# Half-product units in a hybrid encoder step: weight sums on GpSimd alone, stored sums on the vector engine, one load queue, more buffers for the last merges

## The chip, the cores and the metric

One core of a Trainium2 chip runs the whole program. The metric is the device time of one execution in microseconds; the median of several executions is compared. In the text PE is the tensor engine, DVE the vector engine, ACT the scalar engine, POOL GpSimd, and SP the engine that only issues transfers; SPq and ACTq are the instruction streams of SP and ACT where they issue transfers.

## The reference

One layer of a streaming encoder for a prompt of 1024 rows and 8 streams of 16 rows (T = 1152 rows together, width 1024). An input projection feeds two branches, a state-space branch (width 2048) and an attention branch (width 1024). The part that the change touches comes after both:

```
u   = gate_m * (y_m @ w_br_m) + gate_a * (y_a @ w_br_a)      # y_m: T x 2048, y_a: T x 1024
out = u @ w_out                                              # T x 1024 @ 1024 x 1024
y   = layer_norm(alpha * x + out, ln_g, ln_b)
```

All of it is in float32 precision: each operand is split into a rounded high part and the remainder, and a product is three matmuls (high by high, high by low, low by high).

## The kernel before, in words

Everything is held transposed: channels on the 128 partitions, rows along the free axis, in three chunks of 384 rows (`ch(0)` to `ch(2)`). The last 415 us of the program, which the change touches, run in this order.

1. `quarter(A0, evac_0)`: the first half of the attention product, 24 outputs of 12 matmuls.
2. `unit(0, steps_0)`: the first half of the state-space product, by a scheme in the manner of Strassen. Its weights come in four pairs `p` (0 to 3; the second unit has 4 to 7). Each pair has four raw weight halves B11, B21, B12, B22 and four differences T1, T2, T4, T3 of them, so eight pieces; they are used in 11 products of 12 matmuls, into 9 PSUM banks, of which 8 can be open at a time.
3. `quarter(A1, evac_1)`: the second half of the attention product. Its results go to DRAM (`pa_d`). Beside it `load_sums(1)` scales the rows of the second unit and makes their sums.
4. `unit(1, steps_1)`: the second half of the state-space product. Its differences T are not made here: `sums_of_weights`, a generator that runs beside the first unit, made them, split them, and stored them in DRAM (`t_d`). Beside this unit, the generator `seconds` loads the two attention halves and their gate (`pa_d`, `gate_d`) for the chunks 0 and 1 and merges them; `final` loads the other gate (tile `gm`) and `finish` merges it into `acc`.
5. The output product with `w_out` and the normalisation: for chunk 0 the sum over `k` is outermost, and `late` merges chunk 2 of `acc` meanwhile, with loads by `load_late`; then chunks 1 and 2.

A piece is made ready by `prepare()`, one piece per step and three ahead of its use: for a raw half ACT casts the high part (L1484) and POOL subtracts for the low part (L1485); for a difference an engine subtracts first (`sum_of`, L1419); a stored difference is one DMA from `t_d` (L1481). The tiles `pc` rotate over four slots, so a piece can be cast only when PE is done with the piece four before. The raw halves sit in one tile `wu` (B11, B21) and two tiles `wv` (B12, B22), with no second buffer: the next pair is loaded (`load_pair`, L1407 and L1412) when the last reader of this pair is done. The list `coming` says at which piece a load is issued.

`sums_of_weights` does 16 steps. Each makes a difference on DVE (L1419), casts it on ACT (L1455), subtracts on DVE (L1442) and stores it from SP (L1439, `t_d<-te`). After them it loads the rows of the second attention half (`load_second`, L1467 and L1468), which `rows_c01` and `rows_c2` split (L1626, L1627).

What runs beside the products is paced by `Flow`: a generator yields a number of ticks, and PE's code calls `flow.tick()` twice per product, so a tick is six matmuls. Pacing decides only the order of instructions in each engine's stream; every engine then works through its stream in order, as its semaphores allow. Inside `with tc.manual_schedule():` each engine keeps the order in which the code issues; outside it a list scheduler orders the instructions by its own estimate of times. Before the change both units were inside such a block, `quarter(A1, ...)` and the statements between the second unit and the output product were not.

PSUM is read out by `to` and `put_on` (L1511 a copy by ACT for the first result of an `acc` block, L1513 and L1519 adds by DVE) and in the second unit by a copy into the tile `shared` (L1548).

Of the kernel before, what the change touches and what calls it, by code (L numbers as in the profile page):

```python
# [11 lines left out]
F32 = mybir.dt.float32  # L12
# [7 lines left out]
P = 128  # L20
# [129 lines left out]
def trunk_step(ctx: ExitStack, tc: tile.TileContext, I, O):  # L150
# [1250 lines left out]

    def load_pair(p, which):

        q = sy if p < 4 else ac
        if which == 0:
            t = wp.tile([P, 1024], F32, tag="wr", name=f"wu{p}", bufs=1)
            q.dma_start(t[:], weights_of(p, 0))  # L1407
            raw[p, "B11"], raw[p, "B21"] = t[:, 0:512], t[:, 512:1024]
        else:
            for i, n in enumerate(("B12", "B22")):  # L1410
                t = lazy["raw"].tile([P, 512], F32, tag=f"raw{i}", name=f"wv{p}_{i}", bufs=1)
                q.dma_start(t[:], weights_of(p, 1)[:, 512 * i:512 * i + 512])  # L1412
                raw[p, n] = t[:]
# [8 lines left out]
    def sums_of_weights():  # L1422

        early = {}

        def load(p):
            for j, names in enumerate((("B11", "B21"), ("B12", "B22"))):
                t = mp.tile([P, 1024], F32, tag="yr", name=f"we{p}_{j}", bufs=4)
                sy.dma_start(t[:], weights_of(p, j))
                early[p, names[0]], early[p, names[1]] = t[:, 0:512], t[:, 512:1024]  # L1430

        steps = [(p, i) for p in range(4, 8) for i in range(4)]
        made = {}
        load(4)
        yield 12
        for at in range(len(steps) + 2):
            if at >= 2:
                p, i = steps[at - 2]
                sy.dma_start(t_d[4 * (p - 4) + i], made[at - 2][1][:].bitcast(F32))  # L1439
            if 1 <= at <= len(steps):  # L1440
                x, o = made[at - 1]
                ve.tensor_tensor(o[:, 512:1024], x, o[:, 0:512].bitcast(F32), ALU.subtract)  # L1442
            if at < len(steps):
                p, i = steps[at]
                x = sum_of(early, p, SUMS[i], ve)
                o = ap.tile([P, 1024], F32R, tag=("ahi0", "alo0", "ahi1", "alo1")[i], name=f"te{p}_{i}")
                made[at] = (x, o)
                if i == 1:
                    if p < 7:
                        load(p + 1)  # L1450
                    else:
                        load_second(0)
                        load_second(1)
                yield 1.4
                ac.copy(o[:, 0:512], x)  # L1455
                yield 1.4
        load_second(2)
        load_second(3)
        yield 3

    rows2 = []

# [10 lines left out]
    def prepare():  # L1473

        n = len(pieces)
        if n >= lazy["limit"]:
            return
        p, name = n // 8, PIECES[n // 8][n % 8]
        t = wp.tile([P, 1024], F32R, tag=("wh", "wl")[n % 2], name=f"pc{n}")
        if p >= 4 and name in SUMS:  # L1480
            ac.dma_start(t[:].bitcast(F32), t_d[4 * (p - 4) + SUMS.index(name)])  # L1481
        else:
            out = sum_of(raw, p, name, ve if p else po) if name in SUMS else raw[p, name]
            ac.copy(t[:, 0:512], out)  # L1484
            po.tensor_tensor(t[:, 512:1024], out, t[:, 0:512].bitcast(F32), ALU.subtract)  # L1485
        pieces.append(t)
        if p % 4 < 3:
            for which, last, gap in ((0, "T4", 1), (1, "T3", 1)) if p < 4 else ((0, "B21", 2), (1, "B22", 3)):
                if name == last:
                    coming.append((n + gap, p + 1, which))  # L1490
        while coming and coming[0][0] <= n:
            load_pair(*coming.pop(0)[1:])
# [12 lines left out]
    def unit(v, steps):  # L1505
# [16 lines left out]
        for p in range(4):  # L1522
# [11 lines left out]
            for at, piece in enumerate(order):  # L1534
                prepare()
                if p == 3:
                    if at == 3:
                        fetch()
                    if at == 6:
                        split()  # L1540
# [93 lines left out]

    def steps_0(p, piece):

        if p == 3 and piece == "B12":
            flow.drain()
            lazy["rows"] = first_rows(1)
        if p == 3 and piece == "B22":  # L1640
            rows_c2()
# [14 lines left out]
        ac.copy(t, d)  # L1656
        ac.dma_start(pa_d[1, j][:, ch(c)], t)

    flow.start(load_sums(1, lazy["rows"]))
    quarter(A1, evac_1, lambda: unit_first(1))  # L1660
    flow.drain()

    G, U, wraw, pending, wo = {}, {}, {}, [], {}

    def seconds():

        xts = {}

        def load(j):
            G[j] = mp.tile([P, T], F32, tag="yr", name=f"pa{j}", bufs=4)  # L1670
            xt = xts[j] = ap.tile([P, 4 * CW], F32, tag=f"ahi{j % 2}", name=f"pb{j}")
            sy.dma_start(G[j][:, 0:2 * CW], pa_d[0, j][:, 0:2 * CW])
            sy.dma_start(xt[:, 0:2 * CW], pa_d[1, j][:, 0:2 * CW])
            sy.dma_start(xt[:, 2 * CW:], gate_d[8 + j][:, 0:2 * CW])

        load(0)
        load(1)
        yield 6
        for j in range(8):
            g, x, t = G[j][:, 0:2 * CW], xts[j][:, 0:2 * CW], xts[j][:, 2 * CW:]  # L1680
            yield 5
            ve.tensor_tensor(g, g, x, ALU.add)
            yield 1
            ve.scalar_tensor_tensor(g, t, 1.0, g, ALU.add, ALU.mult)
            if j < 6:
                load(j + 2)
            yield 5

    def final(*jcs):

# [13 lines left out]

    def load_late(j):

        for tag, src in (("gt", pa_d[0, j]), ("gt", pa_d[1, j]), ("s4", gate_d[8 + j]), ("s4", gate_d[j])):
            t = mp.tile([P, CW], F32, tag=tag, name=f"lt{j}", bufs=2)
            sy.dma_start(t[:], src[:, ch(2)])
            pending.append(t[:])  # L1710

    def late(j):

        x0, x1, ta, tm = (pending.pop(0) for _ in range(4))
        a = acc[:, j, ch(2)]
        po.tensor_tensor(x0, x0, x1, ALU.add)
        ve.scalar_tensor_tensor(x0, ta, 1.0, x0, ALU.add, ALU.mult)
        ve.scalar_tensor_tensor(a, tm, 1.0, a, ALU.add, ALU.mult)
        po.tensor_tensor(a, a, x0, ALU.add)
        if j < 7:  # L1720
            load_late(j + 1)

    def parts_of_u(c, ks):

# [58 lines left out]
    raw_stack.close()  # L1783
    op = ma_stack.enter_context(tc.tile_pool(name="op", bufs=1, reuse_waits="tile"))
    wo[0] = ready.pop(0)
    split_wo(2)
    lazy["seventh"]()
    split()
    wo[1] = ready.pop(0)
    load_wo(6)  # L1790
    parts_of_u(0, (3,))
    split_wo(3)
    parts_of_u(0, (4, 5))
    finish(2)
    load_late(0)
    rows_of_wo = (0, 2, 1, 3, 4, 5, 6, 7)
    gb = xp.tile([P, 2, D], F32, tag="xhi2", name="gb")
    sy.dma_start(gb[:, 0, :], I["ln_g"].to_broadcast([P, D]))
# [1 line left out]
    for c in range(NCH):  # L1800
# [20 lines left out]
        if c == 0:  # L1821
            for k in range(8):
                for j, n in blocks:
                    product(j, n, k)
                if k < 4:
                    split_wo(k + 4)
                if k == 0:
                    parts_of_u(0, (6, 7))
                if k == 2:
                    load_wo(7)  # L1830
                if k > 2:
                    late(k - 3)
            parts_of_u(1, range(8))
# [119 lines left out]
```

## Time and profile before

| | us |
|---|---|
| median of 3 executions | 2034.54 (2033.39 to 2042.21) |
| the profiled execution, its own time | 2032.59 |
| its span, first to last instruction | 2030.8 |
| PE busy | 2004.2 |
| DVE, ACT, POOL busy | 1358.9, 950.6, 545.5 |

Busy time of PE counts matmuls from a modelled start to a modelled end and says nothing on the rate inside; the number of matmuls in a stretch of time does. A row of the timeline gives the start in us, the duration in us, engine, line, operation, output and inputs, and in brackets how long the engine had been idle before it and what released it. SPq and ACTq rows are transfers being issued; their duration is the issue, not the transfer.

### The profile page before, as it was taken

What the parts mean: (1) busy time and instruction counts of PE and PEld (TensorE: products, weight loads), DVE (VectorE), ACT (ScalarE), POOL (GpSimd) and SP (SyncE); (2) the same over time, 40 slices, a digit from 0 to 9 for tenths busy, and PEclk for the clock granted to TensorE, in tenths of its full rate; (3) what the DMA queues carried; (4) which work ended last, traced back from release to release, by engine and by line L of the source; (5) the groups of instructions that cost most, each with busy time, mean ns of one, the idle gap of its engine ahead of it and who ended that gap; (6) DMA issues with size and microseconds to landing.
All of it is one profiled execution on the core that took longest, in us unless ns stands there. A gap on an engine that the chain in (4) does not pass through costs nothing. (4 is left out here: it accounts for less than half of the span.)

```text
span 2030.8 us, 36480 instructions
## 1 busy us (share of the span) xinstructions
PE 2004.2 (99%) x14199; PEld 1855.9 (91%) x14199; DVE 1358.9 (67%) x2229; ACT 950.6 (47%) x2059; POOL 545.5 (27%) x724
## 2 busy tenths in 40 slices
PE   9999999999999999999999999999999999899998
PEld 7899999999999999999898888988988999799977
DVE  4145666666767667643678777777786677765777
ACT  5125455564555655533555645545445463451310
POOL 0012535353535454423010010001001014413430
PEclk9999999999999999999999999999999999999999
DMA  7423242324332332334566656566566676677853
GB/s 222 166 66 94 69 136 79 131 77 124 95 126 83 127 99 99 124 123 145 167 191 197 201 206 201 186 220 199 174 214 209 216 255 227 206 241 274 286 165 125
DMA packets 139180, 332.37 MB, mean 164 GB/s; under 512 B 20360, under 2 KB 80256, under 8 KB 128768
## 3 DMA queue, kind: packets, MB, share of 16 engines
q1 hardware_dynamic: 117392, 226.17, 34.6%
q10 hardware_dynamic: 21616, 103.88, 14.8%
q8 instruction: 111, 1.82, 0.4%
q14 instruction: 61, 0.50, 0.1%
HBM read 255.66 MB, written 74.33 MB: 162 GB/s over the span
## 5 line engine op out<-in xcount | busy, mean ns | idle before, releaser
L247 PE MATMUL d<-xh,wh 128*128 128x384 f32 x2112 | 736.2, 349 | 0.0
L249 PE MATMUL d<-xh,wl 128*128 128x384 f32 x2112 | 708.3, 335 | 0.0
L248 PE MATMUL d<-xl,wh 128*128 128x384 f32 x2112 | 707.2, 335 | 0.0
L247 PEld LDWEIGHTS d<-xh,wh 128*128 128x128 f32 x2112 | 396.7, 188 | 19.0 <-issue 8.3
L248 PEld LDWEIGHTS d<-xl,wh 128*128 128x128 f32 x2112 | 397.2, 188 | 0.8
L249 PEld LDWEIGHTS d<-xh,wl 128*128 128x128 f32 x2112 | 396.5, 188 | 0.0
L227 POOL TENSOR_TENSOR wl<-wr,wh 128x1024 fp32r<-128x1024 f32 x37 | 90.6, 2447 | 182.9 <-ACT wh L226 182.9
L958 ACT ACTIVATE st<-s,ckt 128x256 f32<-128x256 f32 (+1 forms) x320 | 115.2, 467 | 18.7 <-PE s L953 16.4
L1018 ACT ACTIVATE st<-st 128x1024 f32<-128x1024 f32 x80 | 83.2, 1062 | 40.8 <-DVE st L1013 37.7
L962 POOL TENSOR_TENSOR st<-st,mask_bf 128x256 f32<-128x256 f32 x64 | 49.5, 794 | 194.5 <-ACT st L958 194.4
L707 ACT ACTIVATE m<-ce,nacum 128x128 f32<-128x128 f32 x288 | 96.9, 392 | 5.7 <-PE y L738 5.7
L230 DVE SCALAR_TENSOR_TENSOR wl<-wr,wh 128x1024 fp32r<-128x1024 f32 x50 | 63.7, 1274 | 32.5 <-ACT wh L229 32.4
L634 POOL TENSOR_TENSOR wx<-xdt,wdt 128x256 f32<-128x256 f32 x72 | 54.0, 751 | 84.8 <-DVE xdt L632 84.8
L226 ACT CAST wh<-wr 128x1024 fp32r<-128x1024 f32 x48 | 50.4, 1049 | 51.0 <-PE d L248 44.4
L1485 POOL TENSOR_TENSOR pc<-wu,pc 128x512 fp32r<-128x512 f32 x28 | 37.7, 1358 | 122.2 <-ACT pc L1484 122.2
L1028 PE MATMUL o<-st,vt 128*64 128x256 f32 (+1 forms) x640 | 68.4, 362 | 0.3
L1028 PEld LDWEIGHTS o<-st,vt 128*64 128x64 f32 x640 | 43.1, 137 | 25.8 <-issue 2.5
L853 ACT ACTIVATE gate<-d,bcol 128x384 f32<-128x384 f32 x48 | 27.7, 578 | 72.4 <-PE d L249 47.2
L687 POOL TENSOR_TENSOR S<-S,ea 128x256 f32<-128x256 f32 x56 | 37.8, 674 | 75.8 <-DVE S L688 64.6
L1039 DVE TENSOR_TENSOR st<-st 128x1024 f32<-128x1024 f32 (+1 forms) x40 | 57.4, 1435 | 0.8
L229 ACT ACTIVATE wh<-wr 128x1024 fp32r<-128x1024 f32 x50 | 52.7, 1054 | 10.8 <-PE d L248 10.8
L335 PE MATMUL v<-vh,xh 128*128 128x512 f32 x144 | 57.1, 397 | 0.0
(929 smaller groups left out, 4348.7 us busy)
## 6 DMA issues: line engine op xcount, KB each, us to landing
wr<-in_wt SPq DMA_DIRECT2D x88, 512.0 KB
kc<-in_cache_k ACTq DMA_DIRECT2D x32, 1024.0 KB
vc<-in_cache_v ACTq DMA_DIRECT2D x32, 1024.0 KB
ce<-ac_d SPq DMA_DIRECT2D x96, 192.0 KB
sb<-cs_d ACTq DMA_DIRECT2D x16, 576.0 KB
yr<-ym_d SPq DMA_DIRECT2D x16, 576.0 KB
gate_d<-gate SPq DMA_DIRECT2D x45, 192.0 KB
s<-in_state_ssm SPq DMA_DIRECT2D x8, 1024.0 KB
```

Source lines behind the costliest of these rows:

```text
L227: lazy.get("sub", po).tensor_tensor(lo[:, :cols], raw[:, :cols], hi[:, :cols].bitcast(F32), ALU.subtract)
L230: ve.scalar_tensor_tensor(lo[:, :cols], raw[:, :cols], scale, hi[:, :cols].bitcast(F32), ALU.mult, ALU.subtract)
L247: te.matmul(out, wh, xh, start=(k == 0), stop=False)
L248: te.matmul(out, wh, xl, start=False, stop=False)
L249: te.matmul(out, wl, xh, start=False, stop=(k == n - 1))
L335: te.matmul(d, xh, wh, start=(k == 0), stop=False)
L634: po.tensor_tensor(wx[b][:], xdt[b][:], wdt[:, b, hs][:, :, None].to_broadcast([P, 4, 64]), ALU.mult)
L707: ac.activation(m[:, j, :], ce[:, j * P:(j + 1) * P], AF.Abs, bias=nacum[:, b, h:h + 1])
L958: ac.activation(S[j][:, e, kb, q0:], ps2[:, e, 256 * x + q0:256 * x + 256], AF.Identity, bias=ckt[:, kb, 2 * hp + e:2 * hp + e + 1])
L1018: ac.activation(w, w, AF.Exp, scale=-1.0)
L1028: te.matmul(o[64 * e:64 * e + 64, 256 * at + q0:256 * at + 256], vt[:, kb, 64 * e:64 * e + 64], S[j][:, e, kb, q0:256], start=(kb == 0), s ...
L1039: ve.tensor_tensor(s[:, :, 0:h, :], s[:, :, 0:h, :], s[:, :, 2 * n - h:2 * n, :], ALU.add)
```

## The change

In the first unit: `sum_of` runs on POOL for every pair (before, for pairs 1 to 3 on DVE). In `sums_of_weights` the cast of the high part moves from ACT to DVE, directly behind the difference; the first wait falls from 12 to 8 ticks, a step from 2.8 to 2.6, and there are 5 ticks more after the last store. `flow.drain()` and `first_rows(1)` come after piece T2 of pair 3 instead of after B12, and the `fetch()` of the next weights one piece later.

In the second attention quarter: manual order.

In the second unit: the loads of raw halves and of the stored differences are issued by SP instead of ACT; the load of the next B11/B21 is issued two pieces later; `seconds` starts its loads 6 ticks later, then takes 9 ticks for a block instead of 11, and waits 2 ticks between the last read of a tile and the load that reuses it.

At the output: the statements between the unit and the product get manual order, and `load_late` has a second set of buffers, so that the loads of one merge are issued while the merge before it is at work.

```
     def load_pair(p, which):
-        q = sy if p < 4 else ac
+        q = sy
...
         load(4)
-        yield 12
+        yield 8
         for at in range(len(steps) + 2):
...
-                yield 1.4
-                ac.copy(o[:, 0:512], x)
-                yield 1.4
+                ve.tensor_copy(o[:, 0:512], x)
+                yield 2.6
+        yield 5
         load_second(2)
         load_second(3)
-        yield 3
+        yield 2
...
         if p >= 4 and name in SUMS:
-            ac.dma_start(t[:].bitcast(F32), t_d[4 * (p - 4) + SUMS.index(name)])
+            sy.dma_start(t[:].bitcast(F32), t_d[4 * (p - 4) + SUMS.index(name)])
         else:
-            out = sum_of(raw, p, name, ve if p else po) if name in SUMS else raw[p, name]
+            out = sum_of(raw, p, name, po) if name in SUMS else raw[p, name]
...
-            for which, last, gap in ((0, "T4", 1), (1, "T3", 1)) if p < 4 else ((0, "B21", 2), (1, "B22", 3)):
+            for which, last, gap in ((0, "T4", 1), (1, "T3", 1)) if p < 4 else ((0, "B21", 4), (1, "B22", 3)):
...
                 if p == 3:
-                    if at == 3:
+                    if at == 4 - v:
                         fetch()
...
     def steps_0(p, piece):
-        if p == 3 and piece == "B12":
+        if p == 3 and piece == "T2":
             flow.drain()
             lazy["rows"] = first_rows(1)
...
-    flow.start(load_sums(1, lazy["rows"]))
-    quarter(A1, evac_1, lambda: unit_first(1))
-    flow.drain()
+    with tc.manual_schedule():
+        flow.start(load_sums(1, lazy["rows"]))
+        quarter(A1, evac_1, lambda: unit_first(1))
+        flow.drain()
...
+        yield 6
         load(0)
         load(1)
-        yield 6
+        yield 4
         for j in range(8):
             g, x, t = G[j][:, 0:2 * CW], xts[j][:, 0:2 * CW], xts[j][:, 2 * CW:]
-            yield 5
+            yield 4
             ve.tensor_tensor(g, g, x, ALU.add)
             yield 1
             ve.scalar_tensor_tensor(g, t, 1.0, g, ALU.add, ALU.mult)
+            yield 2
             if j < 6:
                 load(j + 2)
-            yield 5
+            yield 2
...
     def load_late(j):
-        for tag, src in (("gt", pa_d[0, j]), ("gt", pa_d[1, j]), ("s4", gate_d[8 + j]), ("s4", gate_d[j])):
-            t = mp.tile([P, CW], F32, tag=tag, name=f"lt{j}", bufs=2)
-            sy.dma_start(t[:], src[:, ch(2)])
-            pending.append(t[:])
+        if j % 2:
+            x = wp.tile([P, 1024], F32, tag="wr", name=f"lx{j}", bufs=1)
+            at = [x[:, 0:CW], x[:, CW:2 * CW]] + [op.tile([P, CW], F32, tag=f"lt{i}", name=f"lt{j}_{i}")[:] for i in range(2)]
+        else:
+            at = [mp.tile([P, CW], F32, tag=("gt", "s4")[i // 2], name=f"lt{j}_{i}", bufs=2)[:] for i in range(4)]
+        for t, src in zip(at, (pa_d[0, j], pa_d[1, j], gate_d[8 + j], gate_d[j])):
+            sy.dma_start(t, src[:, ch(2)])
+            pending.append(t)
...                                      # late(j)
-        if j < 7:
-            load_late(j + 1)
+        if j < 6:
+            load_late(j + 2)
...
     wo[0] = ready.pop(0)
-    split_wo(2)
...
+    with tc.manual_schedule():
+        split_wo(2)
+        lazy["seventh"]()
+        split()
+        wo[1] = ready.pop(0)
+        load_wo(6)
+        parts_of_u(0, (3,))
+        split_wo(3)
+        parts_of_u(0, (4, 5))
+        finish(2)
+        load_late(0)
...
                 if k == 2:
                     load_wo(7)
+                if k == 1:
+                    load_late(1)
```

More of the change, by code (lines that the diff above doesn't have):

```diff
@@ L1785, in trunk_step @@
     wo[0] = ready.pop(0)
-    split_wo(2)
[L1787 to L1795, printed above, removed]
+    with tc.manual_schedule():
[9 more added lines that the diff above has]
+        load_late(0)
     rows_of_wo = (0, 2, 1, 3, 4, 5, 6, 7)
```

## Prediction

> **What bounds the kernel now.** First the page's head, then the windows by stage, then the list of waits of PE.
>
> ```profile
> span 2030.8 us, 36480 instructions
> ...
> PE 2004.2 (99%) x14199; PEld 1855.9 (91%) x14199; DVE 1358.9 (67%) x2229; ACT 950.6 (47%) x2059; POOL 545.5 (27%) x724
> ```
>
> PE is never free for long: 26.6 us of the span are without a matmul. So nothing can be won beside PE; only holes in PE's stream can close. The windows (columns: PE busy and matmul count, then PEld, DVE, ACT, POOL, granted clock, DMA share, GB/s) say where the holes are.
>
> ```profile
> 1615.40:1665.40 50.00, 50.00 (x291) 50.00 (x290) 41.16 (x64) 29.95 (x65) 2.54 (x2) 1.00 0.78 272
> 1665.40:1767.10 101.70, 94.86 (x529) 91.27 (x528) 70.01 (x95) 42.86 (x86) 49.84 (x35) 1.00 0.60 212
> 1767.10:1820.30 53.20, 50.61 (x290) 49.85 (x289) 43.33 (x62) 29.14 (x61) 11.60 (x6) 1.00 0.68 221
> 1820.30:1848.90 28.60, 24.85 (x134) 24.44 (x133) 9.62 (x16) 5.62 (x11) 5.14 (x4) 0.94 0.78 270
> 1848.90:1917.80 68.90, 68.90 (x398) 68.90 (x397) 46.19 (x70) 11.82 (x21) 28.70 (x22) 1.00 0.80 280
> ...
> 1665.40:1688.30 22.90, 22.90 (x133) 22.90 (x132) 9.92 (x15) 10.32 (x21) 15.66 (x12) 1.00 0.49 173
> ...
> 1917.80:1927.80 10.00, 7.30 (x26) 5.59 (x25) 8.54 (x12) 6.99 (x11) 3.42 (x3) 0.83 0.96 327
> 1927.80:1937.80 10.00, 8.28 (x35) 6.19 (x35) 10.00 (x11) 2.94 (x4) 5.53 (x4) 1.00 0.52 168
> 1937.80:1947.80 10.00, 10.00 (x46) 8.29 (x45) 6.89 (x11) 1.06 (x1) 2.50 (x3) 1.00 0.57 178
> ```
>
> Read as one stage a row: the first attention quarter (clean, 50.0 us), the first unit, the second quarter, the first pair of the second unit, its other three pairs (clean, 22.97 each); then pair 0 of the first unit (clean, 22.9), and three tens of the output product. Lost against the clean rate: the first unit 101.7 - 4 x 22.9 = 10.1; the second quarter 53.2 - 50.0 = 3.2; the second unit's first pair 28.6 - 22.97 = 5.6; the output 20 + 11 matmuls at 10/46 us = 6.7. Together 25.6 us. The whole prediction is how much of these four comes back.
>
> ```profile
> PE u10m L1499 <- ACT sh L1548: 3.8, 1, 3.8
> PE out L1818 <- DVE wl L230: 2.7, 1, 2.7
> PE dq L248 <- DVE ya1lo L1627: 2.2, 1, 2.2
> PE u02m L1499 <- ACT pc L1484: 1.8, 1, 1.8
> ...
> PE out L1817 <- ACT wh L229: 1.6, 1, 1.6
> ```
>
> Each loss has a name: pieces late in the first unit (`pc`), a late low part of the rows (`ya1lo`), one long wait at the start of the second unit, two late splits of `w_out`. The two longest cost more than the wait: after them the clock column falls (0.94, 0.83), and 5.6 us are lost for 3.8 waited.
>
> **First unit.** Four edits meet here: differences of pairs 1 to 3 on POOL (12 instructions move), 16 casts from ACT to DVE, the earlier start, the order of SP's loads.
>
> ```profile
> 1673.70 1.29 POOL L1419 TENSOR_TENSOR wu<-wv,wu 128x512 f32<-128x512 f32 x1
> 1675.73 1.29 POOL L1485 TENSOR_TENSOR pc<-wu,pc 128x512 fp32r<-128x512 f32 x1 [0.73 <-ACT pc L1484]
> 1676.98 1.29 POOL L1419 TENSOR_TENSOR wu<-wu 128x512 f32<-128x512 f32 x1
> ...
> 1755.59 1.27 POOL L1485 TENSOR_TENSOR pc<-wu,pc 128x512 fp32r<-128x512 f32 x1 [2.27 <-ACT pc L1484]
> ```
>
> Pair 0 already has its differences on POOL: one piece takes 1676.98 - 1673.70 = 3.28 us there (difference, cast by ACT, remainder). A pair then loads POOL with 15.7 of 22.9 us, and pair 0 lost nothing. So POOL itself fits. What made pairs 2 and 3 late shows on SP and DVE.
>
> ```profile
> 1729.25 9.98 SPq L1439 DMA_DIRECT2D t_d<-te  x4
> ...
> 1741.64 0.85 SPq L1412 DMA_DIRECT2D wv<-in_wbr  x2
> ...
> 1746.55 0.69 DVE L1419 TENSOR_TENSOR wu<-wv,wu 128x512 f32<-128x512 f32 x1 [3.55 <-DMA wv<-in_wbr]
> ```
>
> SP stands 10 us in the stores of the finished steps, because DVE is late with them, and the load of `wv` for pair 3 is queued behind the last store (1739.2) and the four row loads. It is issued at 1741.6 and in use at 1746.55; the third difference of that pair is ready at 1755.59 + 1.27 = 1756.9, and the unit ends 10.2 us later. So the unit ends 27.9 us after the last store, or after 91.6 us if that is later. The queue order is unchanged (row loads, then `wv`), and three pieces at 3.28 us on POOL take 9.8 us against 10.3 here, so the rule holds after: without loss the last store has to leave 63.7 us into the unit; before it was 73.8.
>
> When will it leave? Before, DVE's part:
>
> ```profile
> L1442 DVE TENSOR_TENSOR te<-we,te 128x512 fp32r<-128x512 f32 x16 | 17.4, 1090 | 10.8 <-ACT te L1455 10.5
> L1419 DVE TENSOR_TENSOR wu<-wv,wu 128x512 f32<-128x512 f32 x6 | 4.1, 682 | 3.8 <-DMA wv<-in_wbr 3.6 <-POOL pc L1485 0.3
> L1513 DVE TENSOR_TENSOR acc<-acc,u01m 128x384 f32<-128x384 f32 x10 | 5.0, 541 | 0.0
> L455 DVE TENSOR_SCALAR pl<-pl 128x432 f32<-128x432 f32 x7 | 2.7, 385 | 0.2
> ...
> 1704.33 1.29 POOL L1485 TENSOR_TENSOR pc<-wv,pc 128x512 fp32r<-128x512 f32 x1 [1.84 <-ACT pc L1484]
> ...
> 1704.35 1.81 DVE L1442 TENSOR_TENSOR te<-we,te 128x512 fp32r<-128x512 f32 x1
> ```
>
> Taken away: 10.5 us in which DVE stood waiting for ACT's casts, 12 differences of 0.68 us (8.2, of which about 9 fall before the last store: 6.1), and about 4 us by the start 4 ticks earlier (a tick is six matmuls, 1.04 us). Added: 16 copies. No row has a 128x512 copy on DVE; the nearest is one-input work on 128x432 at 0.385, which scales to 0.46, and two-input work of the same size is 0.68: 7.4 to 10.9 us; I take 0.46, since the copy has one input. Added too: waits for POOL. The last two rows show it: POOL starts at 1704.33, DVE's remainder 0.02 us later takes 1.81 instead of 0.68, that is, it ran when POOL was done. On average the remainders wait 1.09 - 0.68 = 0.41 us. POOL's share of the time rises from 49.84/101.7 to about 15.7/22.9, by 1.4, so 0.16 us more on each of 32 instructions (5 us), and 0.57 on each copy (9 us) if a copy waits as well, none if it doesn't. Sum: -10.5 - 6.1 - 4 + 7.4 + 5 + (0 to 9) = -8 to +1 us. I take the middle, -4. Ends for the range: -10 (all lost time), and +5, if POOL's waits double once more.
>
> The Trainium skill, "SBUF — State Buffer", section "Who interferes with whom", makes this a rule: a vector instruction with two SBUF inputs and a GpSimd instruction that reads SBUF hold a shared port pair in turn, each for its whole length, and a copy can enter the mode that needs the pair too. The trace agrees (1.81 against 0.68 us). By that rule the copies wait as well, and the sum here is the upper end, about +1 instead of -4.
>
> ACT loses 16 casts, and its in-order stream no longer ties the pieces to DVE; that is why I expect no new loss in pairs 1 and 2.
>
> **Second quarter.** Lost 3.2, of which 2.2 for `ya1lo`.
>
> ```profile
> 1756.88 0.33 SPq L214 DMA_DIRECT2D wr<-in_wbr  x1
> ...
> 1757.73 0.43 SPq L1341 DMA_DIRECT2D rsb<-rs_d  x1
> ...
> 1763.82 5.37 DVE L1345 SCALAR_TENSOR_TENSOR yr<-yr,mcol,rsb 128x1152 f32<-128x1152 f32 x2 [0.93 <-DMA rsb<-rs_d]
> ...
> 1773.00 3.07 DVE L1627 TENSOR_TENSOR ya1lo<-yc,ya1hi 128x384 fp32r<-128x384 f32 x2
> ...
> 1772.69 2.50 POOL L227 TENSOR_TENSOR wl<-wr,wh 128x1024 fp32r<-128x1024 f32 x1 [4.72 <-ACT wh L226]
> ```
>
> The rows' loads stood behind `fetch` (1756.88, held until the raw weights were free), so scaling began at 1763.82 and pushed `ya1lo` to 1773, where it also met POOL. After, the loads come two pieces earlier and ahead of `fetch`, and the casts of the last rows are issued ahead of the quarter's own. `fetch` moves behind two row loads and a broadcast, but it waits for the raw tile anyway. Forcing the order can also cost: ACT's read-outs stand in one line with the casts, but eight banks give 16 us. I take -2.5 (bounds -3.2 and +3, one wait of today's size doubled).
>
> **Second unit.**
>
> ```profile
> 1818.46 0.33 ACTq L1657 DMA_DIRECT2D pa_d<-pa  x1
> 1824.15 0.34 ACTq L1412 DMA_DIRECT2D wv<-in_wbr  x1
> ...
> 1828.60 0.44 ACTq L1481 DMA_DIRECT2D pc<-t_d  x1
> ```
>
> ACT stood 5.7 us at the issue of `wv`, whose tile was still being written to `pa_d`, and the first stored piece, the casts of the rows and the copy `sh` all came behind it: `pc<-t_d` left at 1828.60, PE needed it at 8.3 us into the unit (1828.6). After, SP issues these, ACT has its read-outs first, and `seconds` loads only 7 ticks later. The last store to `pa_d` can leave about 1 us after the quarter's end, so the piece leaves some 3 us into the unit and has 5 us to land, about what `wv` took above. I take -5.5 of 5.6. What is now queued on SP: every stored piece stands behind the merge loads and `gm` loads. A piece is issued three pieces, 8.3 us at least, ahead of use; a merge block is 1.2 MB, at 280 GB/s 4.2 us, and the piece itself 0.5 MB, 1.9 us. 6.1 of 8.3: the cover is 2.2 us, and if SP also waits for a free tile longer than that, PE waits. Blocks come every 9 ticks instead of 11, so DMA's 0.80 rises to about 0.85. Bounds: -5.6, and +6 (2 us at each of three pairs). The later load of B11/B21 has 6.3 us before its cast: nothing.
>
> **Output.**
>
> ```profile
> 1905.53 8.74 SPq L1737 DMA_DIRECT2D wor<-in_w_out  x2
> ...
> 1919.31 2.01 DVE L230 SCALAR_TENSOR_TENSOR wl<-wr,wh 128x1024 fp32r<-128x1024 f32 x1
> ...
> 1931.23 1.05 ACT L229 ACTIVATE wh<-wr 128x1024 fp32r<-128x1024 f32 x1
> ```
>
> The last merges of `seconds` (11 ticks a block) were drained in a lump, DVE was late, `wl` came at 1919.31 although PE was there at 1917.8; the next raw `w_out` could only be loaded after it, and its split at 1931.23 made the second hole. After, the last merge is issued at tick 79 instead of 84, 9 ticks a block; DVE has two instructions less in the last pair. Then `wl` is done before the unit ends and the load of the next raw tile has 8 us. I take -6 of 6.7, with -2 as the poor end. The second set of late buffers shortens merges that no hole in PE waits for: nothing, unless a bank is late; the last normalisation stays.
>
> **Sum.** -4 - 2.5 - 5.5 - 6 = -18. The profiled execution (2032.59; span 2030.8 and 1.8 around it) goes to 2014.6; its time lies 2.0 under the median, on which the forecast is made: 2034.5 - 18 = 2016.5.
>
> **Rivals.**
> 1. DVE and POOL take turns so often that the first unit gets nothing back or loses up to 5. For it: the 1.81 us row. Against: pair 0. Time 2034.5 - 14 + (0 to 5) = 2020.5 to 2025.5.
> 2. SP's single queue: stored pieces late in pairs 1 to 3. For: SP stood 8.74 and 9.98 us in single waits above; against: these pairs were clean with a DMA share of 0.80. +12 (4 us a pair): 2028.5, no measurable change. The same time comes if the forced order changes nothing because the waits move by a few us only.
> 3. Slower: DVE becomes the bound of the first unit by running out of banks. Its adds stand in line with the 48 instructions of the stored sums; nine banks are used in 22.9 us, so eight give it 20 us less the product's own 2, 18. If each of the 48 waits out a whole POOL instruction (1.29 + 0.6), a step takes 5.7 us and the adds of that time (10 of 0.54 us in 22.9) bring it to 7.4: 16 steps, 118 us, issued within 43; 118 - 43 - 18 = 57 us more than the clean 91.6, 47 more than before, and 2034.5 + 47 - 14 = 2067.5. It decides for slower by 10 us from 24 us net, a step of (24 + 10 + 43 + 18) / 16 = 5.9 us. Before, with the last store at 73.8 us, a step took at most 4.6.
>
> **How the numbers follow.** Half a per cent, 10 us, is about what a measurement of this kernel can tell from no change. The forecast's case (2007 to 2020): 0.57. Rival 1: 0.20, still faster. Rival 2 and no effect: 0.17, within. Rival 3: 0.06. So faster 0.77, same 0.17, slower 0.06. The lower end is all 25.6 us: 2009, less 2 for the spread of the median: 2007. The upper end takes rival 1 and part of rival 2: 2027.
>
> **What the profile after would show.** Right: no `pc` wait over 1 us in the first unit and the last `t_d<-te` leaving by 70 us into it; no wait of `u10m` and no clock under 1.00 in the second unit; `wl` done before the first `out`. Wrong: DVE remainders of 1.3 us and more throughout, adds 18 us behind their product; PE waiting for DMA `pc<-t_d` in pairs 5 to 7; a new wait of the quarter on ACT.

## The result, and the profile after

The changed kernel took 2026.99 us (median of 8 runs, 2024.26 to 2029.41) beside 2037.22 us for the kernel before on the same chip: ratio 0.9946, 95% interval 0.9931 to 0.9961. Measured once more (`e_after_again`) it took 2025.78 beside 2034.80: ratio 0.9959, 0.9946 to 0.9971. So 9 to 10 us were gained, where 18 were forecast. The median lies 0.01 us under the upper end of the forecast's range of 2007 to 2027. Head and busy time of the page after:

```profile
span 2025.7 us, 36480 instructions
...
PE 2004.6 (99%) x14199; PEld 1857.2 (92%) x14199; DVE 1371.2 (68%) x2233; ACT 944.6 (47%) x2043; POOL 566.0 (28%) x736
```

DVE has 12 us more work than before, POOL 20 more, ACT 6 less. The windows, one stage a row: first unit, second quarter, second unit, output (columns as before: PE, PEld, DVE, ACT, POOL, granted clock, DMA share, GB/s).

```profile
1667.70:1772.10 104.40, 96.89 (x530) 94.12 (x530) 87.75 (x103) 34.70 (x71) 71.08 (x47) 0.97 0.60 207
1772.10:1826.30 54.20, 51.74 (x290) 51.42 (x289) 40.67 (x59) 30.20 (x62) 10.90 (x5) 0.97 0.65 203
1826.30:1918.90 92.60, 92.07 (x529) 91.78 (x529) 59.27 (x88) 15.98 (x29) 35.88 (x28) 1.00 0.86 307
1918.90:2018.40 99.50, 99.03 (x482) 83.50 (x480) 75.51 (x135) 19.31 (x36) 23.67 (x19) 1.00 0.52 175
```

Against before: first unit 104.4 (101.7), quarter 54.2 (53.2), second unit 92.6 (97.5), output 99.5 (105.7). The two late stages gave what was forecast; the first unit and the quarter went the other way. What PE waits for:

```profile
PE u03d L1499 <- ACT pc L1484: 4.5, 1, 4.5
PE dq L249 <- POOL wl L227: 2.5, 1, 2.5
PE u02m L1501 <- POOL pc L1485: 2.1, 2, 1.1
...
PE u10m L1499 <- DMA pc<-t_d: 0.5, 1, 0.5
```

Of the long wait at `u10m` (3.8) 0.5 us are left; the waits at `ya1lo` (2.2) and `w_out` (2.7, 1.6) are gone. New are 4.5 us at `u03d`, the first piece of pair 3 of the first unit, and 2.5 us at the low part of the last weights of the quarter. The first one's cause stands in SP's stream and on ACT:

```profile
1728.68 10.91 SPq L1439 DMA_DIRECT2D t_d<-te  x4
1739.68 0.38 SPq L1407 DMA_DIRECT2D wu<-in_wbr  x1
...
1742.48 0.86 SPq L1412 DMA_DIRECT2D wv<-in_wbr  x2
...
1744.76 0.62 ACT L1484 CAST pc<-wu 128x512 fp32r<-128x512 f32 x1 [8.34 <-DMA wu<-in_wbr]
```

The load of pair 3's `wu` is queued behind the last four stores, and SP stands 10.9 us in these. Before, the same load was issued at 1728.81, ahead of them. The quicker pacing of `sums_of_weights` moved the stores forward in SP's stream, but DVE did not get quicker:

```profile
L1442 DVE TENSOR_TENSOR te<-we,te 128x512 fp32r<-128x512 f32 x16 | 18.0, 1122 | 0.2
L1454 DVE CAST te<-we 128x512 fp32r<-128x512 f32 x16 | 17.5, 1094 | 0.5
L1419 DVE TENSOR_TENSOR we<-we 128x512 f32<-128x512 f32 x8 | 9.8, 1230 | 0.0
L1419 DVE TENSOR_TENSOR we<-we,we 128x512 f32<-128x512 f32 x8 | 8.9, 1106 | 0.1
...
1711.84 1.39 DVE L1454 CAST te<-we 128x512 fp32r<-128x512 f32 x1
1715.98 0.43 DVE L1454 CAST te<-we 128x512 fp32r<-128x512 f32 x1
...
1711.51 2.87 POOL L1485 TENSOR_TENSOR pc<-wu,pc 128x512 fp32r<-128x512 f32 x2 [0.26 <-ACT pc L1484]
```

Of the two casts shown, the one beside an idle POOL took 0.43 us and the one beside a busy POOL 1.39; the mean of the 16 is 1.094. The stored sums cost DVE 54.2 us, and there is no idle time left among them.

### The profile page after: what moved, and what is told of

Its sections match the earlier page's. It is cut to its first block, busy times and chain, and to the rows that moved or that the text cites. A ratio compares the mean times of both kernels' runs of the same rounds, so it can differ in the third digit from the quotient of the medians.

```text
span 2025.7 us, 36480 instructions
## 1 busy us (share of the span) xinstructions
PE 2004.6 (99%) x14199; PEld 1857.2 (92%) x14199; DVE 1371.2 (68%) x2233; ACT 944.6 (47%) x2043; POOL 566.0 (28%) x736
## 4 chain that ended last, share of the span: by engine, by line
PE 83%; DVE 9%; DMA 2%; ACT 2%; issue 2%; POOL 1%; ACTq 0%; SPq 0%; DVEq 0%; POOLq 0%
PE d L247 17%; PE d L249 16%; PE d L248 16%; PE s L953 3%; PE o L1028 2%; PE y L738 2%; PE v L336 2%; PE v L337 2%; PE out L1826 2%; PE out L1827 2%; PE out L1825 2%; PE v L335 2%; PE so L1103 1%; PE dS L679 1%; PE y L742 1%
## 5 line engine op out<-in xcount | busy, mean ns | idle before, releaser
L958 ACT ACTIVATE st<-s,ckt 128x256 f32<-128x256 f32 (+1 forms) x320 | 115.5, 467 | 17.7 <-PE s L953 13.4
L226 ACT CAST wh<-wr 128x1024 fp32r<-128x1024 f32 x48 | 50.5, 1051 | 52.7 <-PE d L248 44.6
L944 POOL MEMSET st<- 128x256 f32 x32 | 9.9, 310 | 172.0 <-DVE fs L1042 172.0
```

The source lines that it names most:

```text
L958: ac.activation(S[j][:, e, kb, q0:], ps2[:, e, 256 * x + q0:256 * x + 256], AF.Identity, bias=ckt[:, kb, 2 * hp + e:2 * hp + e + 1])
```

## The experiments

Two theories went in. A: the first unit lost because the last stores, timed by a DVE that waits for POOL, stand ahead of pair 3's loads on SP. B: POOL's chain of difference and low part is too slow, so pieces are late whatever SP does. Each row below is a kernel; stage lengths are from one stage's first matmul to the next one's in its profiled execution, "last store" counts from the first unit's start, and ratios are against the kernel before on the same chip.

| kernel | ratio (95%) | first unit | last store | quarter | second unit | output |
|---|---|---|---|---|---|---|
| before | 1 | 101.7 | 73.8 | 53.2 | 97.5 | 105.7 |
| changed | 0.9946 (0.9931 to 0.9961) | 104.4 | 71.9 | 54.2 | 92.6 | 99.5 |
| e_after_again | 0.9959 (0.9946 to 0.9971) | 103.4 | 71.4 | 52.0 | 93.7 | 99.5 |
| e_stores_last | 0.9956 (0.9941 to 0.9971) | 101.3 | 71.3 | 54.4 | 94.1 | 99.5 |
| e_pace_old | 0.9983 (0.9974 to 0.9993) | 105.1 | 75.3 | 55.1 | 95.8 | 99.5 |
| e_act_cast | 0.9926 (0.9911 to 0.9941) | 97.5 | 65.2 | 52.4 | 95.7 | 99.5 |
| e_dve_sums | 0.9952 (0.9935 to 0.9969) | 103.2 | 69.3 | 55.4 | 92.7 | 99.5 |
| e_cast_dve | 0.9922 (0.9906 to 0.9939) | 96.1 | 62.6 | 54.9 | 92.6 | 99.5 |
| e_quarter_pace | 0.9937 (0.9923 to 0.9952) | 101.6 | 70.7 | 51.2 | 93.6 | 99.5 |
| e_cast_td | 0.9925 (0.9911 to 0.9940) | 97.5 | 64.4 | 53.7 | 91.8 | 99.5 |
| e_best | 0.9896 (0.9882 to 0.9911) | 98.8 | 65.7 | 49.9 | 91.8 | 99.5 |
| e_best_dve | 0.9896 (0.9882 to 0.9909) | 95.9 | 61.0 | 50.5 | 91.8 | 99.5 |
| e_merges_old | 0.9981 (0.9972 to 0.9991) | 105.1 | 72.8 | 54.6 | 98.1 | 99.6 |
| e_queue_late_old | 1.0017 (1.0007 to 1.0026) | 103.2 | 72.3 | 58.5 | 97.6 | 102.2 |

The first unit of one and the same instruction stream (changed, e_after_again, e_quarter_pace, e_merges_old, e_queue_late_old) ran 101.6 to 105.1 us, mean 103.5; a difference of 1 or 2 us between single rows of that column proves nothing. The first unit of the kernel before was profiled once, so its spread is not known.

**e_stores_last.** Only the last four stores move, behind the load of pair 3's `wu`.

```
-            if at >= 2: ...                  # one store a step
+            if 2 <= at < 14: store(at - 2)
...
         yield 5
+        for n in range(12, 16): store(n)
         load_second(2)
```

> Only edit to the changed kernel: the last four stores of the early differences (t_d) are issued five steps later, so that on SP the load wu of pair 3 stands ahead of them instead of behind. Theory (the order on SP made the loss): wu is issued at about 1728.7 instead of 1739.7 us, PE's 4.5 us wait at u03d and the 0.8 us and half-rate matmuls (about 3 us) behind it go; the first unit falls from 104.4 to about 96.5 us and the time by about 7.5 us to some 2019.5 us. Rival (GpSimd's differences are the late ones): a wait of 2 to 4 us turns up at pair 3's T pieces (POOL as releaser) and the unit stays at 102 to 104 us, the time at 2025 to 2027.

Measured: the wait at `u03d` vanished as A has it, and the unit still took 101.3. Issue order on SP, then POOL and PE's waits:

```profile
1727.53 0.33 SPq L1407 DMA_DIRECT2D wu<-in_wbr  x1
1727.96 9.58 SPq L1437 DMA_DIRECT2D t_d<-te  x4
1739.96 0.85 SPq L1412 DMA_DIRECT2D wv<-in_wbr  x2
...
1745.66 1.27 POOL L1419 TENSOR_TENSOR wu<-wv,wu 128x512 f32<-128x512 f32 x1 [7.22 <-DMA wv<-in_wbr]
...
PE u03m L1507 <- POOL pc L1491: 2.5, 3, 1.6
...
PE u03m L1505 <- ACT pc L1490: 1.4, 1, 1.4
```

The waits moved to pair 3's T pieces, as B has it, but the row of POOL shows why: it stood idle 7.2 us for `wv`, which is still behind the stores. So in the changed kernel both loads of pair 3 stand behind the last store, and to move one is worth at most some 2 us of the unit, within the spread, and nothing that the ratio shows. That gives theory A a sharper form: what counts is when the last store leaves, and not only which loads stand behind it.

**e_pace_old.** The pacing alone back (start after 12 ticks, 2.8 a step).

```
-        yield 8
+        yield 12
...
-                yield 2.6
-        yield 5
+                yield 2.8
...
-        yield 2
+        yield 3
```

> Only edit: the pacing of the early differences is that of the kernel before (a start of 12 ticks, 2.8 a step, 3 at the end, no pause of 5). This puts wu of pairs 1, 2 and 3 and wv of pair 2 back to where the kernel before had them on SP; casts stay on VectorE, first differences on GpSimd. Theory: wv of pair 2 too is no longer behind stores, so the 1.2 and 1.3 us holes of pair 2 shrink as well: first unit 95 to 97 us, time 2018 to 2020 us. Rival (GpSimd and VectorE take turns, so GpSimd's differences are late): holes at POOL's pieces stay as in the kernel before, first unit 100 to 104 us, time 2023 to 2027.

A miss for both: 105.1 us. `wu` of pair 3 was ahead of the last four stores, but behind the four before, and all of them ran later:

```profile
1719.70 13.34 SPq L1439 DMA_DIRECT2D t_d<-te  x4
...
1735.42 0.38 SPq L1407 DMA_DIRECT2D wu<-in_wbr  x1
1735.90 6.83 SPq L1439 DMA_DIRECT2D t_d<-te  x4
```

The last store left 75.3 us into the unit, 3.4 later than in the changed kernel. That is what the pacing as a whole is worth to the store; the prediction counted its earlier start at 4 us. The order on SP that the theory wanted did not come about, so this run doesn't price it.

**e_act_cast.** The cast of the stored sums back on ACT.

```
-                ve.tensor_copy(o[:, 0:512], x)
+                ac.copy(o[:, 0:512], x)
```

> Only edit: the cast of the stored differences back on ScalarE, with the changed kernel's pacing and SP order. Theory (VectorE's pace, held up by GpSimd, times the stores that wu waits behind): VectorE loses 0.43 to 1.40 us a step, sixteen times, so the last store leaves some 8 to 15 us sooner (57 to 64 us into the unit instead of 71.9), wu of pair 3 with it, and the 4.5 us hole goes: first unit 96 to 98 us, time 2019 to 2021. Rival (the order on SP holds wu whatever VectorE's pace, or ScalarE's own queue delays the piece casts): hole stays at 3 to 5 us, first unit 102 to 105 us, time 2025 to 2028.

Measured as A had it: 97.5 us, last store at 65.2 instead of 71.9 (57 to 64 expected), no wait at `u03d`, although SP's order is that of the changed kernel. DVE's sums of that kernel:

```profile
L1442 DVE TENSOR_TENSOR te<-we,te 128x512 fp32r<-128x512 f32 x16 | 17.3, 1082 | 7.7 <-ACT te L1454 7.7
L1419 DVE TENSOR_TENSOR we<-we,we 128x512 f32<-128x512 f32 x8 | 11.7, 1464 | 0.1
L1419 DVE TENSOR_TENSOR we<-we 128x512 f32<-128x512 f32 x8 | 10.9, 1364 | 0.0
```

17.5 us of casts leave, 3.9 us come back on the differences (18.7 to 22.6; that they now meet POOL more often is the likely reason), and 7.5 us of idle time behind ACT: 6 us in all, nearly what the last store moved. ACT's wait, whose removal the prediction booked as 10.5 us, costs less than the casts that removed it.

**e_dve_sums** and **e_cast_dve.** The differences of pairs 1 to 3 back on DVE, first in the changed kernel, then in e_act_cast.

```
-            out = sum_of(raw, p, name, po) ...
+            out = sum_of(raw, p, name, ve if p else po) ...
```

> Only edit: the differences of pairs 1 to 3 of the first unit back on VectorE (GpSimd keeps pair 0 and the low parts). Theory: VectorE has twelve more instructions of 0.7 us or more, the last store leaves later than 71.9 us into the unit by 3 to 8 us, and wu of pair 3 behind it: the hole at u03d grows from 4.5 to 8 us or more; first unit 107 to 113 us, time 2030 to 2036. Rival (taking turns with GpSimd is the whole loss): with fewer GpSimd instructions VectorE's casts run at 0.43 us, the stores leave earlier, the hole shrinks; first unit 98 to 102 us, time 2021 to 2025.

> The cast on ScalarE (as in e_act_cast) and the differences of pairs 1 to 3 on VectorE as in the kernel before; what is left of the first unit's edits is the pacing alone. Theory (GpSimd's chain of difference and low part is too slow for pair 1's single-product pieces, and moving the differences to it buys little once the stores leave early): first unit within 2 us of e_act_cast's 97.5 us, pair 1's 1.4 and 1.3 us waits smaller, last store at 65 to 69 us into the unit. Rival (GpSimd's differences are what frees VectorE in time): last store at 70 us or later, first unit 100 to 103 us.

The first is a miss for both forecasts: with twelve more instructions on DVE the last store left sooner (69.3), not later, and the unit took 103.2. The hole at `u03d` is gone, but PE now waits 3.9 us at pair 1's `u01m` and 2.1 at pair 3's `u03m`. POOL has less to do, and DVE's rows are shorter:

```profile
L1454 DVE CAST te<-we 128x512 fp32r<-128x512 f32 x16 | 15.6, 973 | 0.5
L1442 DVE TENSOR_TENSOR te<-we,te 128x512 fp32r<-128x512 f32 x16 | 15.3, 955 | 0.2
```

That is 4.6 us less on these two rows, and 3.0 on the differences of the stored sums. Against 12 x 0.68 = 8.2 us of added work, moving the differences to POOL freed DVE of next to nothing. The unit's 103.2 lies within the spread of the changed kernel's. With the cast on ACT the same edit gave 96.1, last store at 62.6, earlier than either forecast had it, and e_best_dve repeats it (95.9 against 98.8 in e_best). Four cells, mean first unit:

| | differences on POOL | on DVE |
|---|---|---|
| cast on DVE | 103.5 (5 executions) | 103.2 (1) |
| cast on ACT | 97.9 (3) | 96.0 (2) |

The cast costs 6 to 7 us, the differences 0 to 2, and what is left of the first unit's edits (start, ticks, earlier row loads) gains 5.7 on the 101.7 before.

In these two kernels the last store leaves at 62.6 and 61.0, ahead of the 63.7 us by which the prediction had a unit without loss, 91.6. The unit still takes 96: the waits left are at pair 1's pieces, most of them for POOL's low part (1.3 at `u01d`). So theory B fits pair 1, and the last store isn't all of the loss.

**e_quarter_pace.** The row sums of the second quarter wait 5 ticks instead of 4 per half block.

```
-            yield 4
+            yield 4 + v                      # at both places; v is 1 in the second half
```

> Only edit to the changed kernel: the row sums of the second quarter wait 5 ticks instead of 4 after each half block, so that on ScalarE the cast that splits the u=3 weights stands ahead of one more half block of row casts. Theory (ScalarE comes to that cast late because the row casts ahead of it wait for VectorE): the 2.5 us wait at the u=3 weights and the half-rate matmuls behind it (1.6 us) go, quarter from 54.2 to 50.5 to 51.5 us, time 3 us shorter, some 2024. Rival (VectorE's 8.7 us a block is itself the pace, so the later blocks are late instead): the wait only moves, to the end of the quarter or into the second unit's first pieces; the two together stay within 1 us of 146.8 us, time 2026 to 2028.

The wait at the u=3 weights (the last ones of the quarter) is gone, quarter 51.2 (1.0 of it at `ya1lo`), and 49.9 and 50.5 in the two kernels that have the edit with the cast on ACT, against 52.0 to 55.4 in the nine others that keep the second unit's loads on SP. In the changed kernel that cast was issued late, and POOL's remainder was long:

```profile
1807.73 1.06 ACT L226 CAST wh<-wr 128x1024 fp32r<-128x1024 f32 x1 [0.40 <-ACT pa L1656]
...
1808.87 3.56 POOL L227 TENSOR_TENSOR wl<-wr,wh 128x1024 fp32r<-128x1024 f32 x1 [14.32 <-ACT wh L226]
```

1807.73 is 35.6 us into the quarter; in e_quarter_pace the same cast starts at 1799.24, 31.9 us into it, and POOL's remainder takes 2.39. The next wait, the second unit's first stored piece, is 1.5 us here; in the two profiles of the changed kernel it is 0.5 and 1.6.

**e_cast_td.** e_act_cast, and the first stored piece's load ahead of `wv` on SP.

```
+        prepare()
         if v:
             load_pair(4, 1)
-        prepare()
```

> The changed kernel with the cast of the stored differences on ScalarE (as in e_act_cast) and, new, the load of the second unit's first stored piece issued ahead of wv of pair 4 on SP. Theory (in e_act_cast that piece is 2.1 us late because on SP it stands behind wv, which waits until the quarter's last results are stored): the 2.1 us wait at u10m and its half-rate matmuls go, second unit from 95.7 to about 93 us, time about 2.5 us below e_act_cast, some 2016.5. Rival (the piece waits for its buffer and for the DMA engines, whatever the order): the wait stays over 1.5 us, time 2018 to 2020.

In e_act_cast the piece stood behind a `wv` that waited until a quarter's result was stored:

```profile
1820.12 2.22 SPq L1412 DMA_DIRECT2D wv<-in_wbr  x2
1822.39 1.46 SPq L1481 DMA_DIRECT2D pc<-t_d  x3
...
PE u10m L1499 <- DMA pc<-t_d: 2.1, 1, 2.1
```

With the edit that wait is in no list, and the second unit takes 91.8 in all three kernels that have it: the clean rate. The ratio did not move (0.9925 against 0.9926), though the second unit is 3.9 us shorter; its quarter was 1.3 longer in the one execution profiled, the profiled execution of e_act_cast lies 3.0 above that kernel's median, and each interval reaches 3 us either way.

**e_best** and **e_best_dve.** The three edits together; the second also has the differences back on DVE.

> All three: cast on ScalarE, stored piece ahead of wv, row sums at 5 ticks. If the three waits are separate (first unit's wu, u=3 weights, first stored piece), the gains add: first unit 97.5, quarter 50.5 to 51, second unit 93, output 99.5; time some 2014.5 us. If the row sums' pace is VectorE's own, the quarter gains nothing: 2016.5 to 2017.5.

> e_best with the differences of pairs 1 to 3 on VectorE as in the kernel before: of the first unit's edits only the pacing is left. Theory (both moves of work in the first unit cost time, GpSimd's chain of difference and low part being what made e_best's 1.9 and 1.3 us waits of pair 1): first unit 96 to 97 us against 98.8, the other stages as in e_best (50, 92, 99.5); time some 2 us below e_best, 2012. Rival (VectorE's extra 8 us comes out again at the rows of the second quarter, as the 0.9 us wait at ya1lo in e_cast_dve): quarter 51.5 or more, time as e_best within 1 us.

The three waits are separate, as the first forecast has it: 2014.28 and 2012.75 us, ratio 0.9896 for both, 20 and 22 us below the kernel before; e_best_dve is 13.0 below the changed one on the same chip (2025.78). The stages add up as expected, but the times don't tell the two kernels apart. What is left of PE's waits in e_best_dve from the first unit on:

```profile
PE u01d L1501 <- POOL pc L1485: 1.3, 1, 1.3
...
PE out L1826 <- DVE wolo L1752: 0.5, 1, 0.5
PE u01d L1499 <- ACT pc L1484: 0.4, 1, 0.4
PE dq L248 <- DVE ya1lo L1627: 0.3, 1, 0.3
```

**e_merges_old.** The merges beside the second unit paced as before (loads at once, 11 ticks a block).

```
-        yield 6
         load(0)
         load(1)
-        yield 4
+        yield 6
...
-            yield 4
+            yield 5
...
-            yield 2
             if j < 6:
                 load(j + 2)
-            yield 2
+            yield 5
```

> Only edit to the changed kernel: the merges in the second unit are paced as in the kernel before (loads at once, 11 ticks a block instead of 9, last merge at tick 84 instead of 79). Theory (the earlier last merges are what lets the weights of the output product be split in time): the output stage goes from 99.5 back to 103 to 106 us, with waits for wl and wh at its start; time 4 to 6 us longer, some 2028 to 2033. Rival (the written order of the output's start, or the second late buffers, made the gain): output stays within 1 us of 99.5.

The output stayed at 99.6: the rival is right, the earlier last merge alone is not what mended the output. The two splits of `w_out` that were late before are in time or nearly so here (PE waits 0.5 us for `wl`):

```profile
1923.20 2.04 DVE L230 SCALAR_TENSOR_TENSOR wl<-wr,wh 128x1024 fp32r<-128x1024 f32 x1
...
1928.97 1.06 ACT L229 ACTIVATE wh<-wr 128x1024 fp32r<-128x1024 f32 x1 [0.30 <-issue]
```

PE began the output at 1923.9, so these start 0.7 us ahead of it and 5.1 behind it; in the kernel before (1919.31 and 1931.23, with PE at 1917.8) it was 1.5 and 13.4 behind. But the second unit went to 98.1, which neither theory had:

```profile
1834.60 0.32 SPq L1481 DMA_DIRECT2D pc<-t_d  x1
...
1843.08 0.66 PE L1499 MATMUL u10m<-ym1h,pc 128*128 128x384 f32 x1 [3.96 <-DMA pc<-t_d]
```

With the merge loads issued at once, the third stored piece stands behind two blocks of them on SP, leaves at 1834.60 and is late by 4 us. In the changed kernel it left with the first two, from 1829.41. So the merges' new pacing is what makes the single queue harmless.

**e_queue_late_old.** The second unit's loads back on ACT's queue, and one set of late buffers.

```
-        q = sy
+        q = sy if p < 4 else ac
...
-            sy.dma_start(t[:].bitcast(F32), t_d[4 * (p - 4) + SUMS.index(name)])
+            ac.dma_start(t[:].bitcast(F32), t_d[4 * (p - 4) + SUMS.index(name)])
...                                              # distance 2 instead of 4; one set of late buffers
-        if j < 6:
-            load_late(j + 2)
+        if j < 7:
+            load_late(j + 1)
```

> The changed kernel with two edits undone that lie in different stages: the second unit's loads back on ScalarE's queue with the old distance (2 pieces), and one set of buffers for the last merges. Theory: the queue is the second unit's gain, so 92.6 goes back to 96 to 98 us with a wait of 2 to 4 us at u10m; the late buffers are worth nothing to PE, so the output stays at 99.5 to 100 us, tail 7.3. Time 4 us longer, some 2030. Rival: output 101 us or more or a longer tail, if the late merges needed the buffers; or second unit at 93 to 94, if the later merge loads and not the queue made its gain.

Second unit 97.6, as expected, and the quarter 58.5, which was not:

```profile
1820.37 0.45 ACTq L1407 DMA_DIRECT2D wu<-in_wbr  x1
1827.79 1.14 ACT L1484 CAST pc<-wu 128x512 fp32r<-128x512 f32 x2 [7.88 <-DMA wu<-in_wbr]
...
PE u10d L1499 <- ACT pc L1484: 4.9, 1, 4.9
```

In the quarter's written order pair 4's `wu` is issued late on ACT, which then stands 7.9 us for it. The two stages together are 156.1 us against 146.8 and 145.7: the one queue, with its load distance, is worth 9 to 10 us to the rest of this change, not 5; the time rose by 12 us over the changed kernel's on the same chip, where 4 were expected. The output was 102.2, with 1.7 us at the second split of `w_out`: its raw tile was asked for at 1925.59 and the cast, held by that load, began at 1936.16. The first split was in time (1923.53, PE at 1926.1). Two edits were undone there, so whether the buffers or the queue delayed the second split stays open.

## Why the prediction was right and wrong

The forecast's own case, 2007 to 2020, did not come, and that 2026.99 lies inside the range is in part luck: the upper end stands on rival 1, which came, and on part of rival 2, which didn't, and a late weight split in the quarter, which is in no term of the sum, took its place.

Of its signs, two of the right ones came (no clock under 1.00 in the second unit; `wl` done at 1918.42, ahead of the first `out` at 1918.9). Against it stand a `pc` wait of 4.5 us in the first unit, the last store at 71.9, `u10m` still waiting, and a new wait of the quarter.

**Second unit** (-5.5, measured -4.9 and -3.8): near in size, and right in cause; the stored piece still waited 0.5 to 1.6 us. Rival 2's mechanism, stored pieces behind merge loads on SP, is real (e_merges_old, 4 us); the pacing inside the same change keeps it away.

**Output** (-6, measured -6.2 twice): size right, by another cause than the prediction gave. It put the gain on the last merge at tick 79; with tick 84 the output stayed at 99.6. With the queue and the buffers undone instead, the first split was still in time. Of the edits that bear on the output's start, what these two kernels share is the order written out there. The rows fit it: in the kernel before, ACT came to the second split 9.9 us after its raw tile was asked for, behind two casts of parts of `u` for which it waited 1.2 and 1.4 us for POOL; in e_merges_old it came to it after 3.7 us. That order was not run alone, and any one of the edits might do, so the cause is argued, not shown.

**Second quarter** (-2.5, measured +1.0 and -1.2): the step "`ya1lo`" was right, that wait is gone. What failed is that nothing was named as late next: the sum took the whole of that wait as gained. The split of the u=3 weights came 35.6 us into the quarter in both kernels; before, PE was held up ahead of it by the `ya1lo` hole and so waited only 0.4 us for it. The bound of +3 held.

**First unit** (-4, measured +2.7 and +1.6): the wrong sign, by two steps, and this is where most of the missing 8 us went.

1. The sum of DVE's terms. The 16 casts were booked at 7.4 us plus 0 to 9 for waits, and the middle taken; they measured 17.5, above the upper end of 16.4. The differences moved off DVE were booked at 6.1 us freed; e_dve_sums shows about none. The last store left 71.9 us into the unit instead of about 70. With what the rows show (idle time -10.6, casts 17.5, longer remainders and sums 3.7) and the start and the moved differences as booked, the sum is +0.5 instead of -4; the store itself moved by -1.9. The sentence on the Trainium skill, "SBUF — State Buffer", section "Who interferes with whom", had the nearer sum: by it a copy can need the port pair that POOL holds, and its sum was the upper end, +1. The rows agree (0.43 against 1.39 us).
2. "The queue order is unchanged". That was checked for `wv`, not for `wu`, which fell behind the four stores. By the rule "27.9 us after the last store" the unit would have been 71.9 + 27.9 = 99.8; it was 104.4. In e_stores_last, with `wu` ahead again, it ended 30.0 after the last store. The rule itself is no constant: in the other changed kernels the unit ended 29.7 to 34.9 us after it.

So rival 1, DVE and POOL in turns with a loss up to 5 us, came in the first unit, with the order of `wu` on SP as a second cause that it doesn't name; its time of 2020.5 to 2025.5 lies just under the medians because the quarter gave nothing either. The whole: -18 was the sum, of which the last two stages gave 10 to 11 in the profiled executions, while the first two gave back up to 3.7. The four stages together gave 7.4 us in the first pair of profiles, but the profiled span moved by 5.1 only, since the changed kernel came to the first unit 2.3 us later, where both programs have the same instructions: the first unit began between 1664.8 and 1668.1 us in the executions here.

## What to carry to other kernels

When pacing moves stores forward in an in-order issue stream, list every load that they pass, not only the one that was late: a store that waits for compute holds all of them. Here the stage got shorter as the last store left earlier, down to some 96 us, where waits for other pieces took over. Work moved between DVE and POOL is not priced by its own rows alone; each instruction moved changes what all the others on both engines wait, so measure the engine's whole block, as the four cells above do. And where a hole in PE's stream is closed, look in each other stream for what was already late behind that hole.

## What the runs showed of the hardware

What a wait costs after it ends varied more than expected. Two windows behind the wait at `u03d` (the granted clock is the third number from the end), in the changed kernel and, after a wait of 4.0 us, in e_quarter_pace:

```profile
1747.00:1750.00 3.00, 3.00 (x10) 3.00 (x11) 3.00 (x3) 0.65 (x3) 2.70 (x2) 0.50 0.89 315
1750.00:1753.00 3.00, 3.00 (x13) 3.00 (x12) 1.37 (x3) 0.91 (x2) 2.35 (x2) 0.60 1.00 360
...
1744.00:1747.00 3.00, 3.00 (x12) 3.00 (x11) 2.00 (x3) 0.22 (x1) 1.93 (x2) 0.59 1.02 358
1747.00:1750.00 3.00, 3.00 (x20) 3.00 (x19) 0.95 (x1) 0.81 (x2) 2.45 (x2) 1.00 0.91 333
```

A clean window of 3 us shows 19 or 20 matmuls by this count. The changed kernel has 10 and 13 in the two windows behind the wait, e_quarter_pace 12 and then the full rate, with the same instructions. Over the five executions of this stream, 48 matmuls from the end of the wait took 1.8 to 3.2 us more than the 8.3 of a clean run, without the waits among them; the longest wait (5.2 us, e_merges_old) cost 2.5, the changed kernel's 4.5 us cost 3.2. The Trainium skill, "TensorE: Matmul & The Clock Gate", section "What's actually happening", tells of a window of about 3.4 us that runs free of the program; that would make the cost a matter of phase, and the rows agree with it, though no run here sets the phase. An idle time shorter than that window is no safe side. The same wait of the second quarter, for the low part `wl`, in e_act_cast and e_cast_td, each with the 3 us behind it:

```profile
1805.49 0.44 PE L249 MATMUL dq<-ya1hi,wl 128*128 128x384 f32 x1 [1.96 <-POOL wl L227]
1805.49:1808.49 3.00, 3.00 (x17) 3.00 (x18) 2.80 (x6) 0.56 (x2) 0.00 (x0) 1.00 0.81 221
...
1805.30 0.55 PE L249 MATMUL dq<-ya1hi,wl 128*128 128x384 f32 x1 [1.98 <-POOL wl L227]
1805.30:1808.30 3.00, 3.00 (x10) 3.00 (x11) 2.79 (x6) 0.54 (x2) 0.00 (x0) 0.53 0.78 212
```

Two waits of equal length before the same matmuls, one at full clock behind it and one at half. In the runs here, from the first unit to the start of the output, 10 of the 30 waits between 1.2 and 2.3 us had a lower clock in the 3 us behind them, and all 13 of 2.46 us or more had. That is one source of the spread between executions of one stream.
